# Two tables' pools become weight places from the third MLP on, and the loads of the S5 layer in another order

## The chip, the cores and the metric

The kernel runs on one core of a Trainium2 chip. The metric is the time of one execution on the device in microseconds, smaller is better. Five engines work beside each other, each through its own instructions in a fixed order: PE (matrix multiply; its weight loads are listed as PEld), DVE, ACT, POOL, and SP, which here only starts transfers. An instruction that has to wait holds back all that stands behind it on its engine.

## The reference

Four layers with a mixer each, and an MLP behind every mixer, on 256 tokens of 1024 channels, all in float32. The change touches the third MLP (`i = 2`) and the mixer after it, S5:

```python
for i in range(DEPTH):
    z = mixer_i(rmsnorm(h, norm_g[i, 0]))
    h = h + rmsnorm(z, norm_g[i, 1])
    z = rmsnorm(h, norm_g[i, 2])
    z = jnp.square(jax.nn.relu(z @ w_up[i])) @ w_down[i]
    h = h + rmsnorm(z, norm_g[i, 3])

def s5_mixer(h, ...):          # 64 groups of 16 channels, 64 complex states each
    bu_re, bu_im = ...         # u through the discretized input matrix
    _, _, xr, xi = lax.associative_scan(combine, (a_re, a_im, bu_re, bu_im), axis=1)
    y = einsum(xr, c_re) - einsum(xi, c_im) + d_skip * u
    y = gelu(y)
    return (y @ w_glu_a) * sigmoid(y @ w_glu_b)
```

## The kernel before

**Weights.** Every float32 product is made of three matmuls (`mm3`, all by line 297), so each weight is split into a high and a low part. A weight tile of 1 MB is loaded by SP (line 116) into one of three `raw` buffers. It is then split in two halves: ACT writes the high part (line 339), DVE the low part (line 340), both into a *place*, a buffer `w` of 8 KB per partition. There are `N_W = 8` places in a pool; a new split takes the place that was given out eight splits earlier, once PE is through with it. `Weights` keeps the order of the tiles (`stream` of each layer), starts the next load when a `raw` buffer has ended (`issue`), and `tick`, called after every unit of matmuls, starts a split when a place has come free by the planner's clock. A tile marked `plain` is not split. With `ahead=True` it is loaded straight into a place.

**The third MLP.** Eight groups `g` of 512 hidden channels: `up_units(g)` multiplies by `w_up` (96 matmuls of 128x256, tiles `mm`), `down_units(g - 1)` by `w_down` (48 matmuls of 128x512, tiles `acc`). A group's `w_up` are two tiles, so four places; so are its `w_down`.

**The tables.** S5's matrices are made on the device while the MLPs run, by a generator (`Tables.work`) whose steps are put between the other work. It uses two pools, `pre` (line 208) and `mp` (line 209). Its results go to DRAM: `d_e`, `d_m` and, in sixteen chunks, `d_f`. Each chunk of `d_f` is made by `into_maps`: six products on DVE (lines 1611 to 1616) from two loads (`pb`, `bt`), and a DMA from POOL's queue (line 1800). Chunks 6 to 15 come beside the third MLP; in `body`, `drain` runs what is left when `g == 6`, between `up_units(6)` and `down_units(5)`.

**S5.** There are four chunks `c` of 16 groups. `into(c)` multiplies by `d_f` chunk `c` and turns the result; `scan(c, v)` rotates it (line 1312), runs a scan in two halves (line 1352), rotates back, and sends it through four matmuls into `x` (line 1367); `within(c)` multiplies by `d_m` (line 1397), `out(c)` by `d_e`, and ACT applies the gelu (line 1409). `turn(0)`, after chunks 0 and 1, transposes and splits the result into `h1hi` and `h1lo`, and the GLU's matmuls can start on its first half. The `d_f` tiles go through the three `raw` buffers, the eight `d_m` and `d_e` through the eight places, and the GLU's weights come after all of them. A block of matmuls on zeros (tile `pf`, `keep_warm`) fills PE's wait ahead of S5.

The order on each engine is set at build time by a scheduler that lists the instructions by its own estimate of time.

Of the kernel before, what the change touches and what calls it, by code (L numbers as in the profile page):

```python
# [31 lines left out]

N_W = 8
N_RAW = 3
LAG = 2.0
# [32 lines left out]
class Tile:  # L68
# [3 lines left out]
    def __init__(self, ap, scale=None, plain=False, shape=None, load=None, ahead=False, gains=None, soon=False):  # L72
        self.gains, self.soon = gains, soon
        self.ap, self.scale, self.plain, self.load, self.ahead = ap, scale, plain, load, ahead
        self.shape = a, b = shape or ap.shape[1:]
        per = max(1, 1024 // b)
        self.cuts = [] if plain else [(i, min(per, a - i)) for i in range(0, a, per)]
        self.raw = None
        self.ended = False
        self.done = 0  # L80
        self.w = []


class Weights:
# [4 lines left out]
    def __init__(self, k):  # L89
# [3 lines left out]
        self.issued = self.current = self.taken = self.started = 0  # L93
        self.freed = []
        self.in_raw = []
# [21 lines left out]

    def place(self):
        self.started += 1
        return self.k.wp.tile([128, 2, 1024], F32R, name="w")  # L120

    def skip_plain(self):

        while self.current < len(self.tiles) and self.tiles[self.current].plain:
            t = self.tiles[self.current]
            if t.ahead:
                if self.started - N_W >= len(self.freed):
                    return
                self.load(t, self.place().bitcast(F32).rearrange("p a b -> p (a b)"))
            self.current += 1  # L130

    def ready(self, clock):

        self.skip_plain()
        if self.current >= self.issued or self.tiles[self.current].plain:
            return False
        j = self.started - N_W
        return j < 0 or (j < len(self.freed) and self.freed[j] <= clock)

    def split(self):  # L140
# [3 lines left out]
        i, m = t.cuts[t.done]  # L144
        assert self.current < self.issued and self.started - N_W < len(self.freed), "weights wait for their own use"
        b = t.shape[1]
        w = self.place()[:, :, 0:m * b].rearrange("p n (a b) -> p n a b", b=b)
        hi, lo = w[:, 0], w[:, 1]
# [11 lines left out]
        self.splits.append(lo_inst.ins)  # L160
        t.w += [(hi[:, e], lo[:, e]) for e in range(m)]
        t.done += 1
        if t.done == len(t.cuts):
# [18 lines left out]
    def free(self, n):  # L182

        self.freed += [self.k.clock] * n

    def free_plain(self, t):
        t.ended = True
        if t.ahead:
            self.free(1)
        self.issue()  # L190


class Core:


    def __init__(self, ctx, tc, a):
# [10 lines left out]
        self.small = pool("small", 6)  # L207
        self.pre_p = pool("pre", 1)
        self.mp = pool("mp", N_MAPS)
        self.dram = pool("dram", 1, space=bass.MemoryType.DRAM)  # L210
        self.pacc = pool("pacc", 4, space=PSUM)
        self.pmm = pool("pmm", 3, space=PSUM)
        self.pf = pool("pf", 1, space=PSUM)
        self.clock = self.credit = self.resume = 0.0
        self.background = None
# [61 lines left out]

    def drain(self):
        while self.background is not None:
            self.step()  # L280

    def run(self, units, side=()):
# [977 lines left out]
class S5(Sublayer):  # L1260
# [10 lines left out]
    def stream(self):  # L1271
        k, add = self.k, self.k.weights.add
        for c in range(4):
            add(k.d_f[:, 16 * c:16 * c + 16], plain=True)
        for c in range(4):
            for maps in (k.d_m, k.d_e):
                add(maps[:, 16 * c:16 * c + 16], plain=True, ahead=True)
        for n in ("d_w_glu_b", "d_w_glu_a"):
            for i in range(0, 8, 2):
                add(rows(self.a[n])[:, i:i + 2], soon=n == "d_w_glu_b" and i < 4)  # L1280

# [23 lines left out]
    def body(self):  # L1305
# [79 lines left out]
        v[3] = into(3)  # L1385
        maps = [k.weights.take() for i in range(8)]
        ys = {}
# [61 lines left out]
        k.tick(1.0)  # L1449
        wb = four()  # L1450
        states(2)
# [536 lines left out]
```

## Time and profile before

| | us |
|---|---|
| time, median of 3 runs | 1065.2 (1063.49 to 1066.76) |
| the profiled execution | 1065.79 |
| its span on the core | 1064.0 |
| PE busy | 1006.6 (95%) |
| DVE, ACT, POOL busy | 746.5, 545.3, 299.6 |
| DMA | 241.30 MB at 227 GB/s |

The profiled execution's own time is its span and 1.8 us around it, and lies 0.6 us over the median. Busy is the time in which an engine has at least one instruction running. PEclk is the share of PE's full clock that was granted: 1.00 is 2.4 GHz, 0.50 is 1.2 GHz. In timelines a row begins with start and duration in us; xN says how many instructions were merged into it, and [t <-X] that the engine stood idle for t before it and what ended that.

### The profile page before, as it was taken

To read this page: it belongs to the slowest core of one execution; us is meant where nothing else is said; L and a number is where in the kernel's file an instruction comes from. 1 tells how busy PE (TensorE), PEld (TensorE's weight loads), DVE (VectorE), ACT (ScalarE), POOL (GpSimd) and SP (SyncE) were. 2 spreads that over 40 slices of the span, in tenths; PEclk is the share of its full clock that TensorE was granted. 3 is DMA by queue.
4 is the path that set the end of the run, shared out by engine and by line. 5 is a ranking of instruction groups with operands and counts; after the bars stand their busy time and mean duration, and the time that the engine had idled before them with its cause. 6 is when DMAs were issued, how large, how long until landed. Compare 5 with 4: busy or idle time off the path is not lost.

```text
span 1064.0 us, 16397 instructions
## 1 busy us (share of the span) xinstructions
PE 1006.6 (95%) x6403; PEld 883.5 (83%) x6403; DVE 746.5 (70%) x1133; ACT 545.3 (51%) x816; POOL 299.6 (28%) x456
## 2 busy tenths in 40 slices
PE   7998999999889999998799999999998999999996
PEld 5886999999679999997688798888966778999995
DVE  5788998856788866579865857666857686455563
ACT  5956545544554454445465654444633656354451
POOL 4010000002118999996600526661100000000000
PEclk9999999999999999999899999999999999999999
DMA  9785557567957877756750889979978454646531
GB/s 315 238 277 171 187 186 235 193 201 256 344 181 249 271 258 242 247 186 220 272 186 21 270 271 311 323 269 318 336 309 301 159 184 160 210 159 206 191 120 39
DMA packets 84589, 241.30 MB, mean 227 GB/s; under 512 B 7408, under 2 KB 9712, under 8 KB 82720
## 3 DMA queue, kind: packets, MB, share of 16 engines
q1 hardware_dynamic: 66192, 180.89, 49.3%
q0 software_dynamic: 17648, 58.78, 16.4%
q8 instruction: 50, 0.82, 0.3%
q10 hardware_dynamic: 672, 0.59, 0.2%
q14 instruction: 27, 0.22, 0.1%
HBM read 220.05 MB, written 28.57 MB: 234 GB/s over the span
## 4 chain that ended last, share of the span: by engine, by line
PE 71%; DVE 9%; DMA 7%; issue 5%; ACT 3%; POOL 3%; DVEq 0%; ACTq 0%; POOLq 0%
PE acc L297 36%; PE mm L297 33%; DVE w L340 3%; DMA d_lag<-lg 2%; DMA d_f<-f 1%; DMA bt<-in_k_bt 1%; DMA bc<-in_norm_g 1%; PE pf L297 1%; ACT w L339 1%; DVE w L338 1%; POOL lg L1861 1%; DVE h L402 1%; ACT junk L353 1%; DMA raw<-in_d_w_glu_b 1%; DMA pb<-d_pb 1%
## 5 line engine op out<-in xcount | busy, mean ns | idle before, releaser
L340 DVE TENSOR_TENSOR w<-raw,w 128x1024 fp32r<-128x1024 f32 (+2 forms) x306 | 379.9, 1266 | 125.4 <-ACT w L339 123.9
L339 ACT ACTIVATE w<-raw 128x1024 fp32r<-128x1024 f32 (+2 forms) x306 | 312.0, 1044 | 211.0 <-PE acc L297 113.4
L297 PE MATMUL acc<-w,h1hi 128*128 128x512 f32 x1280 | 395.2, 392 | 3.1 <-DVE w L340 1.6
L297 PE MATMUL mm<-zhi,w 128*128 128x256 f32 x1920 | 355.2, 284 | 4.0 <-DVE s L853 2.4
L297 PEld LDWEIGHTS mm<-zhi,w 128*128 128x128 f32 x1920 | 303.2, 192 | 7.0 <-DVE s L853 2.6
L297 PEld LDWEIGHTS acc<-w,h1hi 128*128 128x128 f32 x1280 | 238.6, 189 | 53.2 <-DVE w L340 2.5
L297 PE MATMUL mm<-zlo,w 128*128 128x256 f32 x960 | 272.2, 284 | 0.0
L297 PE MATMUL acc<-w,h1lo 128*128 128x512 f32 x640 | 247.7, 392 | 2.8 <-DVE h1lo L340 2.8
L297 PEld LDWEIGHTS mm<-zlo,w 128*128 128x128 f32 x960 | 184.7, 192 | 1.1
L297 PEld LDWEIGHTS acc<-w,h1lo 128*128 128x128 f32 x640 | 120.6, 188 | 29.6 <-DVE h1lo L340 4.1
L339 ACT ACTIVATE h1hi<-s 128x512 fp32r<-128x512 f32 x60 | 45.3, 757 | 57.6 <-DVE s L647 56.0
L646 ACT ACTIVATE s<-mm 128x512 f32<-128x512 f32 x56 | 33.2, 593 | 64.2 <-PE mm L297 62.6
L647 DVE TENSOR_TENSOR s<-s 128x512 f32<-128x512 f32 x56 | 42.7, 763 | 29.2 <-ACT s L646 29.1
L340 DVE TENSOR_TENSOR h1lo<-s,h1hi 128x512 fp32r<-128x512 f32 x60 | 49.7, 830 | 19.0 <-ACT h1hi L339 18.8
L398 DVE TENSOR_TENSOR t<-acc,bc 128x512 f32<-128x512 f32 x28 | 19.2, 688 | 42.4 <-ACT junk L353 42.4
L353 ACT ACTIVATE junk<-acc 128x512 bf16<-128x512 f32 x28 | 16.6, 594 | 59.8 <-PE acc L297 59.6
L297 PE MATMUL mm<-w,zhi 128*128 128x512 f32 x128 | 40.3, 396 | 4.1 <-DVE zlo L340 3.2
L297 PE MATMUL acc<-w,zhi 128*128 128x512 f32 (+2 forms) x128 | 39.0, 384 | 2.4 <-ACT w L337 1.7
L1774 POOL DMA_DIRECT2D d_e<-ec x64 | 40.4, 633 | 0.0
L1749 POOL TENSOR_TENSOR ec<-bo,pr 128x256 f32<-128x256 f32 x32 | 33.6, 1050 | 9.0 <-DMA bo<-in_k_c 8.9
L329 POOL DMA_DIRECT2D bc<-in_norm_g x15 | 8.2, 547 | 97.3 <-DVE v L363 35.2
L1749 POOL TENSOR_TENSOR tmp<-bo,pi 128x256 f32<-128x256 f32 x32 | 32.8, 1025 | 1.1
(318 smaller groups left out, 1067.9 us busy)
## 6 DMA issues: line engine op xcount, KB each, us to landing
raw<-in_w_up SPq DMA_DIRECT2D x64, 1024.0 KB, 5.5
raw<-in_w_down SPq DMA_DIRECT2D x64, 1024.0 KB, 5.2
bc<-in_norm_g POOLq DMA_DIRECT2D x15, 512.0 KB, 5.7
raw<-in_a_w_in SPq DMA_DIRECT2D x7, 1024.0 KB, 10.7
d_ec<-ec POOLq DMA_DIRECT2D x16, 288.0 KB, 2.6
ec<-d_ec POOLq DMA_DIRECT2D x16, 288.0 KB, 6.8
bt<-in_k_bt POOLq DMA_DIRECT2D x16, 256.0 KB, 5.5
raw<-in_a_w_out SPq DMA_DIRECT2D x4, 1024.0 KB, 5.7
```

The lines of the kernel that those rows point to most:

```text
L297: return self.nc.tensor.matmul(out, lhsT, rhs, start=start, stop=stop)
L338: return i, nc.vector.scalar_tensor_tensor(lo, src, gain, hi.bitcast(F32), op0=ALU.mult, op1=ALU.subtract)
L339: i = nc.scalar.activation(hi, src, AF.Copy)
L340: return i, nc.vector.tensor_tensor(out=lo, in0=src, in1=hi.bitcast(F32), op=ALU.subtract)
L353: self.nc.scalar.activation(self.junk[:, 0:x.shape[-1]], x, AF.Square, scale=scale, bias=shift, accum_out=ss[:, i:i + 1])
L398: nc.vector.tensor_tensor(tn, zn, gn, op=ALU.mult)
L402: nc.vector.scalar_tensor_tensor(hn, tn, q, hn, op0=ALU.mult, op1=ALU.add)
L646: nc.scalar.activation(s, state[f], AF.Relu)
L647: nc.vector.tensor_tensor(s, s, s, op=ALU.mult)
L1749: tt = lambda o, x, y, op: nc.gpsimd.tensor_tensor(o, x, y, op=op)
L1774: nc.gpsimd.dma_start(out=k.d_e[64 * r:64 * r + 64, 4 * ch + g:4 * ch + 4:2], in_=e[hs, :, r, 1:9].rearrange("p q i c -> p q (i c)"))
L1861: nc.gpsimd.tensor_copy(v[:, e, 4:7, e], t[:, 1:6:2])
```

## The change

Places become a number that can grow. When the tables are done, `drain` closes their two pools and opens a pool `more` of two places in the memory that they held; from there on two of every ten splits take a place of `more` and the other eight of the old pool. The bookkeeping of free places goes by place number, since `d_f` chunks now end in another order than they were taken. In S5 all `d_f` tiles go into places (`ahead=True`), so the `raw` buffers stay with split weights; the stream puts the GLU's first tile ahead of the last `d_m` and `d_e`, and `body` takes them in that order. The GLU's first tiles are no longer marked `soon`.

```diff
@@ Weights
+    def widen(self, n):
+        self.n, self.more, self.since = N_W + n, n, self.started
+
-    def place(self):
+    def place(self, t):
+        t.places.append(self.started)
+        pool = self.k.more if self.more and (self.started - self.since) % self.n < self.more else self.k.wp
         self.started += 1
-        return self.k.wp.tile([128, 2, 1024], F32R, name="w")
+        return pool.tile([128, 2, 1024], F32R, name="w")
...
     def free(self, n):
-        self.freed += [self.k.clock] * n
+        self.end(self.split_places[0:n])
+        del self.split_places[0:n]
+
+    def end(self, places):
+        self.ends.update((p, self.k.clock) for p in places)
+        while len(self.freed) in self.ends:
+            self.freed.append(max(self.ends[len(self.freed)], self.freed[-1] if self.freed else 0))
...
@@ Core
-        self.pre_p = pool("pre", 1)
-        self.mp = pool("mp", N_MAPS)
...
+        self.made = ctx.enter_context(ExitStack())
+        self.pre_p = self.made.enter_context(tc.tile_pool(name="pre", bufs=1))
+        self.mp = self.made.enter_context(tc.tile_pool(name="mp", bufs=N_MAPS))
...
     def drain(self):
         while self.background is not None:
             self.step()
+        self.made.close()
+        self.more = self.ctx.enter_context(self.tc.tile_pool(name="more", bufs=N_MORE))
+        self.weights.widen(N_MORE)
@@ S5.stream
+        plain = lambda maps, c: add(maps[:, 16 * c:16 * c + 16], plain=True, ahead=True)
+        glu = lambda n, i: add(rows(self.a[n])[:, 2 * i:2 * i + 2])
         for c in range(4):
-            add(k.d_f[:, 16 * c:16 * c + 16], plain=True)
-        for c in range(4):
-            for maps in (k.d_m, k.d_e):
-                add(maps[:, 16 * c:16 * c + 16], plain=True, ahead=True)
-        for n in ("d_w_glu_b", "d_w_glu_a"):
-            for i in range(0, 8, 2):
-                add(rows(self.a[n])[:, i:i + 2], soon=n == "d_w_glu_b" and i < 4)
+            plain(k.d_f, c)
+        for c in range(3):
+            plain(k.d_m, c)
+            plain(k.d_e, c)
+        glu("d_w_glu_b", 0)
+        plain(k.d_m, 3)
+        plain(k.d_e, 3)
+        for i in range(1, 4):
+            glu("d_w_glu_b", i)
+        for i in range(4):
+            glu("d_w_glu_a", i)
@@ S5.body
-        maps = [k.weights.take() for i in range(8)]
+        maps = [k.weights.take() for i in range(6)]
...
-        wb = four()
+        wb = k.weights.take()
+        maps += [k.weights.take() for i in range(2)]
+        wb = wb + k.weights.take()
```

In the program as built, three places move. The first is ACT in the third MLP, at the splits of the last group's `w_up` (`w_7292` to `w_7317` before, `w_7292` to `w_7322` after); in brackets stand the semaphores waited for, where DMASW are the transfers of POOL's queue, DMAHW those of SP's. Before:

```order
L339 ACTIVATE w_7292<-raw_7115 128x1024 [waits DMAHW1_49,PE_49,Activation_49]
L339 ACTIVATE w_7295<-raw_7115 128x1024 [waits PE_49,Activation_49]
L646 ACTIVATE s_7287<-mm_7237 128x512 [waits PE_49]
L339 ACTIVATE w_7300<-raw_7170 128x1024 [waits DMAHW2_49,DVE_49]
L339 ACTIVATE w_7317<-raw_7170 128x1024 [waits DVE_49]
L339 ACTIVATE h1hi_7175<-s_7287 128x512 [waits DVE_49]
```

After:

```order
L361 ACTIVATE w_7292<-raw_7115 128x1024 [waits DMAHW1_49,PE_49,Activation_49]
L361 ACTIVATE w_7295<-raw_7115 128x1024 [waits PE_49,Activation_49]
L668 ACTIVATE s_7287<-mm_7237 128x512 [waits PE_49]
L361 ACTIVATE w_7300<-raw_7170 128x1024 [waits DMAHW2_49,DVE_49]
L361 ACTIVATE h1hi_7175<-s_7287 128x512 [waits DVE_49]
L361 ACTIVATE w_7322<-raw_7170 128x1024 [waits DMASW3_49,DMASW4_49,DMASW2_49,DMASW5_49,DMASW1_49,DMASW6_49,DMASW0_49,DMASW7_49,DVE_49,Pool_49]
L361 ACTIVATE w_7327<-raw_7205 128x1024 [waits DMAHW3_49]
```

The last quarter of these weights is now the first tile in the memory of the tables' pools, and its split has moved behind `h1hi` and waits for all that used that memory.

The second is DVE in S5, from the second chunk's scan to the first half's `h1lo` (`s` are the scan's tiles, `w` splits). Before:

```order
L1352 SCALAR_TENSOR_TENSOR s<-t,s 128x256 x2
L1312 TENSOR_TENSOR s<-s,t 128x512 x2
L340 TENSOR_TENSOR w<-raw,w 128x1024
L1312 TENSOR_TENSOR s<-mm,t 128x512 x2
L340 TENSOR_TENSOR w<-raw,w 128x1024
L1312 TENSOR_TENSOR s<-s 128x256 x2
L1312 TENSOR_TENSOR s<-mm,t 128x512
L340 TENSOR_TENSOR w<-raw,w 128x1024
L340 TENSOR_TENSOR h1lo<-acc,h1hi 128x4x128 x2
```

After:

```order
L1380 SCALAR_TENSOR_TENSOR s<-t,s 128x256
L362 TENSOR_TENSOR w<-raw,w 128x1024
L1380 SCALAR_TENSOR_TENSOR s<-t,s 128x256
L362 TENSOR_TENSOR w<-raw,w 128x1024
L1340 TENSOR_TENSOR s<-s,t 128x512 x2
L1340 TENSOR_TENSOR s<-mm,t 128x512 x2
L1340 TENSOR_TENSOR s<-s 128x256 x2
L362 TENSOR_TENSOR w<-raw,w 128x1024
L1380 SCALAR_TENSOR_TENSOR s<-t,s 128x256 x2
L1340 TENSOR_TENSOR s<-mm,t 128x512
L362 TENSOR_TENSOR w<-raw,w 128x1024
L1340 TENSOR_TENSOR s<-s,t 128x512 x2
```

Two GLU splits now stand inside the second chunk's scan, and behind the rows shown follow one more split and then `h1lo`, with the third chunk's scan ahead of it.

The third is SP's queue around S5. Before:

```order
L116 DMA raw<-d_f 128x2048 x3
L116 DMA w<-d_m 128x2048
L116 DMA w<-d_e 128x2048
...
L116 DMA raw<-d_f 128x2048
L116 DMA raw<-in_d_w_glu_b 128x2x1024 x4
```

After:

```order
L119 DMA raw<-in_d_w_glu_b 128x2x1024 x2
L119 DMA w<-d_f 128x2048 x2
L119 DMA raw<-in_d_w_glu_b 128x2x1024
L119 DMA w<-d_f 128x2048 x2
L119 DMA w<-d_m 128x2048
L119 DMA w<-d_e 128x2048
...
L119 DMA raw<-in_d_w_glu_b 128x2x1024
```

Three of the four tiles of `d_w_glu_b` are now loaded ahead of the maps.

## Rows read from the trace of the kernel before

**Rows 1.** The page, part 1: busy us, share of the span, instructions.

```profile
PE 1006.6 (95%) x6403; PEld 883.5 (83%) x6403; DVE 746.5 (70%) x1133; ACT 545.3 (51%) x816; POOL 299.6 (28%) x456
```

**Rows 2.** Stretches: us, then busy us (instructions) by engine, PEclk, DMA share, GB/s.

```profile
740.00:760.00 20.00, 20.00 (x126) 18.11 (x126) 18.77 (x25) 12.71 (x14) 4.11 (x8) 1.00 0.89 305
780.00:800.00 20.00, 18.54 (x176) 12.05 (x178) 13.81 (x34) 7.11 (x17) 0.62 (x2) 1.00 0.99 403
800.00:820.00 20.00, 16.06 (x255) 12.01 (x248) 15.07 (x23) 8.22 (x14) 0.00 (x0) 1.00 0.81 306
```

**Rows 3.** The chain that ended last, in order of time: start, us, what.

```profile
753.17 11.51 PE mm L297 x96
764.68 21.79 PE acc L297 x96
805.40 6.35 DMA raw<-in_d_w_glu_b
```

**Rows 4.** Timeline of ACT in the third MLP's last groups.

```profile
747.38 2.20 ACT L339 ACTIVATE w<-raw 128x1024 fp32r<-128x1024 f32 x2
749.49 1.18 ACT L339 ACTIVATE h1hi<-s 128x512 fp32r<-128x512 f32 x1
```

**Rows 5.** Timeline of DVE there.

```profile
749.02 2.34 DVE L340 TENSOR_TENSOR w<-raw,w 128x1024 fp32r<-128x1024 f32 x2
751.29 0.41 DVE L1612 TENSOR_TENSOR t<-pb,bt 128x256 f32<-128x256 f32 x1
754.28 0.42 DVE L1616 TENSOR_TENSOR f<-f,t 128x256 f32<-128x256 f32 x1
```

**Rows 6.** Timeline of POOL there: the last chunk of d_f.

```profile
755.00 0.55 POOL L1800 DMA_DIRECT2D d_f<-f  x1 [9.69 <-DVE f L1616]
```

**Rows 7.** DMA issues of d_f at 755.0, 648.1, 709.8: KB, us from issue to landing.

```profile
d_f<-f POOLq DMA_DIRECT2D x1, 256.0 KB, 4.5
d_f<-f POOLq DMA_DIRECT2D x1, 256.0 KB, 3.9
d_f<-f POOLq DMA_DIRECT2D x1, 256.0 KB, 6.9
```

**Rows 8.** Timeline of PE ahead of the first MLP, and stretches as in Rows 2.

```profile
294.10 2.31 PE L297 MATMUL mm<-zhi,t 128*128 128x128 f32 x10 [3.98 <-DVE t L430]
290.00:295.00 5.00, 1.02 (x6) 0.90 (x6) 4.54 (x13) 4.91 (x12) 0.00 (x0) 0.93 1.02 406
295.00:300.00 5.00, 5.00 (x30) 4.90 (x30) 4.96 (x9) 1.29 (x3) 0.55 (x1) 0.72 0.73 244
```

**Rows 9.** Timeline of PE in S5.

```profile
800.67 1.06 PE L1397 MATMUL pf<-w,zlo 128*32 128x128 f32 x32
807.18 1.08 PE L297 MATMUL mm<-s,ident 128*64 128x256 f32 x8 [0.37 <-DVE s L1312]
812.24 0.66 PE L1333 MATMUL mm<-ident,s 128*128 128x128 f32 x4 [1.19 <-ACT s L1329]
814.16 1.20 PE L297 MATMUL acc<-w,h1hi 128*128 128x512 f32 x4 [0.34 <-ACT h1hi L339]
817.40 0.50 PE L297 MATMUL acc<-w,h1lo 128*128 128x512 f32 x1 [2.04 <-DVE h1lo L340]
```

**Rows 10.** Timeline of ACT in S5.

```profile
804.36 0.65 ACT L1367 ACTIVATE t<-mm 128x248 f32<-128x248 f32 x2 [6.09 <-PE mm L297]
805.47 0.60 ACT L1329 ACTIVATE s<-mm 128x512 f32<-128x512 f32 x1 [0.46 <-PE mm L297]
809.69 2.00 ACT L339 ACTIVATE w<-raw 128x1024 fp32r<-128x1024 f32 x2
```

**Rows 11.** Timeline of DVE in S5.

```profile
805.04 1.27 DVE L1352 TENSOR_TENSOR_SCAN s<-t,s 128x256 f32<-128x256 f32 x2
806.34 1.29 DVE L1312 TENSOR_TENSOR s<-s,t 128x512 f32<-128x512 f32 x2
```

**Rows 12.** Timeline of PE at the fourth MLP's start.

```profile
881.89 0.73 PE L297 MATMUL mm<-w,zhi 128*128 128x512 f32 x2 [0.70 <-DVE zlo L340]
```

More of the change, by code (lines that the diff above doesn't have):

```diff
@@ L33 @@
 N_W = 8
+N_MORE = 2
 N_RAW = 3
@@ L78, in __init__ @@
         self.raw = None
+        self.places = []
         self.ended = False
@@ L93, in __init__ @@
         self.issued = self.current = self.taken = self.started = 0
-        self.freed = []
+        self.freed, self.ends, self.split_places = [], {}, []
+        self.n, self.more, self.since = N_W, 0, 0
         self.in_raw = []
@@ L126, in skip_plain @@
             if t.ahead:
-                if self.started - N_W >= len(self.freed):
+                if self.started - self.n >= len(self.freed):
                     return
-                self.load(t, self.place().bitcast(F32).rearrange("p a b -> p (a b)"))
+                self.load(t, self.place(t).bitcast(F32).rearrange("p a b -> p (a b)"))
             self.current += 1
@@ L136, in ready @@
             return False
-        j = self.started - N_W
+        j = self.started - self.n
         return j < 0 or (j < len(self.freed) and self.freed[j] <= clock)
@@ L144, in split @@
         i, m = t.cuts[t.done]
-        assert self.current < self.issued and self.started - N_W < len(self.freed), "weights wait for their own use"
+        assert self.current < self.issued and self.started - self.n < len(self.freed), "weights wait for their own use"
         b = t.shape[1]
-        w = self.place()[:, :, 0:m * b].rearrange("p n (a b) -> p n a b", b=b)
+        w = self.place(t)[:, :, 0:m * b].rearrange("p n (a b) -> p n a b", b=b)
         hi, lo = w[:, 0], w[:, 1]
@@ L161, in split @@
         t.w += [(hi[:, e], lo[:, e]) for e in range(m)]
+        self.split_places.append(t.places[-1])
         t.done += 1
@@ L182, in free @@
     def free(self, n):
-        self.freed += [self.k.clock] * n
+        self.end(self.split_places[0:n])
[4 more added lines that the diff above has]
+            self.freed.append(max(self.ends[len(self.freed)], self.freed[-1] if self.freed else 0))
     def free_plain(self, t):
         t.ended = True
-        if t.ahead:
-            self.free(1)
+        self.end(t.places)
         self.issue()
@@ L213, in __init__ @@
         self.pf = pool("pf", 1, space=PSUM)
+        self.made = ctx.enter_context(ExitStack())
+        self.pre_p = self.made.enter_context(tc.tile_pool(name="pre", bufs=1))
+        self.mp = self.made.enter_context(tc.tile_pool(name="mp", bufs=N_MAPS))
+        self.ctx = ctx
         self.clock = self.credit = self.resume = 0.0
```

## The prediction, made before the changed kernel ran

> **What bounds the kernel now.** First the page's busy times: PE is busy for 95% of the span, the next engine for 70% [rows 1], so time is gained or lost almost only where PE stands still or runs slowly. Then the stretches: in the third MLP's last groups PE is busy for 20.00 of 20 us, in S5 it stands still for 1.46 us of one stretch and 3.94 us of the next [rows 2]. Then the chain that ended last, to see what PE waits for in each place. In the third MLP it is PE itself, 11.51 us for the last group's up product and 21.79 us for the down products behind it, without a gap; in S5 it runs through the load of the GLU's weights [rows 3]. The timelines of the engines there carry the sum.
>
> **A wait where there was none: the third MLP.** The first split that goes into the new memory is the last quarter of the last group's `w_up`, `w_7322`. As built it waits for the tables' pools to be empty, and the last to leave is the DMA that writes the sixteenth chunk of `d_f`: the count waited for on DMASW4 is the one that this DMA raises. When does it land? Before, DVE's products for that chunk begin at 751.29 and the last begins at 754.28 [rows 5]; POOL issues the DMA at 755.00 [rows 6], and it lands 4.5 us later [rows 7], at 759.5. The change takes one low part (2.34 / 2 = 1.17 us [rows 5]) out of DVE's way ahead of these products, but `h1lo` now precedes them and waits for `h1hi`, which follows on ACT when the one high part left of the 2.20 us pair is done [rows 4]. I take 0.9 us earlier: issue at 754.1, landing at 758.6.
>
> PE gets to the last group at 753.17 and takes 11.51 / 96 = 0.120 us a matmul [rows 3]. As built, 18 matmuls stand ahead of the first on `w_7322`, so PE stops at 753.17 + 18 x 0.120 = 755.3. ACT's split takes 2.20 / 2 = 1.1 us [rows 4], so PE goes on at 758.6 + 1.1 = 759.7. **The wait is 4.4 us**, on a stretch in which PE was the chain, so all of it counts. For landing the nearest rows are 3.9 and 6.9 us [rows 7], so the wait is 3.8 to 6.8; I take 4.5, the same chunk's own row. The Trainium skill, "DMA: Bandwidth & Descriptors", section "Anatomy of one DMA — SWDGE (gpsimd) path", gives such a DMA a fixed 2.0 us and its bytes at 436 GB/s, an estimate of 2.6 us for 256 KB; by that the wait would be 2.5 us and the sum 1.9 us smaller. No d_f row of the trace is that short, so the rows decide.
>
> Behind `w_7322` on ACT stand the splits of both last `w_down` pairs and the relu of this group. They are late, but not late enough for a second wait: from 759.7 ACT and DVE need about 1.15 us for each part, the four of the next down product are through at about 765.5, and PE wants them at 764.68 + 4.4 = 769.1. The loads behind them on SP start only when `w_7322`'s `raw` buffer is free, at about 760.9; the splits of the last pair then fall into 767 to 773, and PE wants them 24 matmuls of 21.79 / 96 = 0.227 us after 769.1, at 774.6. That cover is about 1 us at its thinnest (the last `h1hi`, at about 774.5, is wanted 11 matmuls later).
>
> **What the wait does to PE's clock.** After standing still for 3.98 us PE goes on at 294.10 and the granted clock is 0.93 in that stretch and 0.72 in the next [rows 8]; 5 x 0.07 + 5 x 0.28 = 1.75 us of PE's time are lost to the lower of the two levels. A wait of 4.4 us is longer, so I add **1.7 us** (between none, as after the 2.04 us wait in S5, where the stretch shows 1.00 [rows 2, 9], and twice this, if a further wait falls into the slow time).
>
> **The GLU's weights in S5.** What can be gained: ahead of the GLU PE waits 1.19, 0.34 and 2.04 us [rows 9], 3.6 us in all, for ACT and DVE, which have the first GLU splits to make when the load has landed at 811.8 [rows 3]. After the change these weights are there long before. But the order then puts two splits into the second chunk's scan, and that scan is itself on the way to the GLU. In times of before, to which the wait above has to be added: the third chunk's `within` (1.06 us for one, about 0.9 from start to start) no longer stands ahead of the first chunk's last matmuls [rows 9], so the chain starts 0.9 us earlier. ACT copies `x` at 804.36 - 0.9 = 803.5 for 0.65 us, then `s` for 0.5 [rows 10], so it is free at 804.65 and splits until 805.65 (2.00 / 2 [rows 10]). DVE has done the first half of the scan at 804.14 + 0.64 = 804.8 [rows 11], waits for that split, makes its low part (1.15), the second half (0.64), the second split's low part (1.15) and the first product (0.65): 805.65 + 3.6 = 809.25. PE started on this product at 807.18 [rows 9]: **2.0 us later**, and PE stands still for about 3.2 us there.
>
> From there the way to the GLU holds on DVE, as built: six products and a scan for the third chunk (1.3 + 0.7 + 0.65 + 1.3 and 1.27), three more low parts (3 x 1.15) and one `h1lo` (0.65), 9.3 us, and some 1.5 us of waiting for PE's matmuls and ACT's copy, from 809.9 to 820.7. Before, the GLU went on at 817.40 [rows 9], with 2.0 us of the third chunk's matmuls still to do, which after the change are done by then. So the GLU is 820.7 - 817.4 - 2.0 = **1.3 us later**, not 3.6 us earlier. Bounds: the whole 3.6 us gained, or 3 us lost if the half-speed clock and the waits add up. The 3.2 us wait can lower the clock as the one in rows 8 did; part of the slow time lies under ACT and DVE, which set the pace there, so of 1.7 us I count **1.0** (0 to 1.7).
>
> **Edits at nothing.** The third and fourth `d_f` tiles now load when places of the next to last down product come free: 769.1 + 63 x 0.227 = 783.4, ahead of the `d_m` and `d_e`. At the 403 GB/s of [rows 2] a tile of 1 MB takes 2.6 us; the seventh, the third chunk's `d_m`, is there at about 802 and wanted at about 808. If that cover went, each tile late would cost its 2.6 us. The new bookkeeping is done at build time.
>
> **Two places ahead later.** At the fourth MLP's start PE waits 0.70 us for a low part [rows 12]; as built, four down matmuls (4 x 0.227 = 0.9 us) now stand in that gap, their weights being two splits further on: **-0.7 us** (0 to -0.7). Elsewhere in that MLP each split waits for the same use as before, so nothing else moves.
>
> **The sum.** 4.4 + 1.7 + 1.3 + 1.0 - 0.7 = +7.7 us. The profiled execution took 1065.8, so 1073.5; it lies 0.6 over the median of 1065.2, so against the median **1072.9**.
>
> **The rivals.** (1) It does what it is described to do and nothing waits: the splits of the GLU no longer hold PE, -3.6 - 0.7 = -4.3, so 1061. It needs `d_f`'s last chunk to have landed by 755.3 - 1.1 = 754.2, the time at which it is issued; the shortest landing of [rows 7] is 3.9. Only if DVE's products for it ran some 4 us earlier would that decide. For it speaks that DVE's order there is mended by one part; against it all of rows 5 to 7. (2) The wait in the third MLP stands, but S5 gains what rows 9 offer: 4.4 + 1.7 - 3.6 - 0.7 = +1.8, so 1067, no change that can be told. It is decided by DVE in the second chunk: if the first product is there by 807.2 (plus 4.4), as before. Against it stands the order, for it that I have the times of ACT and DVE there only by adding rows. (3) The wait is at its long end, a landing of 6.9 us [rows 7] (+2.4), and the clock falls twice at full price (+0.7), or a low part misses its cover of 1 us (+1): 1077.
>
> **How the numbers follow.** About 0.3%, 3.2 us, is what a measurement of this kernel can tell from no change. Forecast (1070 to 1075.5) 0.60, rival 1 0.06, rival 2 0.18, rival 3 0.16. Faster is rival 1, 0.06; the same is rival 2, 0.18; slower the rest, 0.76. The range leaves out rival 1 and the ends of the others: 1066.5 to 1077.5.
>
> **What would show it.** On ACT, the second split of the pair ahead of `h1hi` gone and a wait of some 8 us for a transfer before the next split, ended by the DMA of `d_f`; on PE, a gap of 4 to 5 us after 18 matmuls of the last group and a granted clock under 1.00 behind it. In S5, DVE's scan halves torn apart by low parts and a PE wait of 3 us ahead of the second chunk's `mm<-s,ident`; the waits charged to GLU splits smaller. Wrong would be: no PE gap before 765 (the whole forecast falls), a gap under 3 us (the landing was mis-sized), or S5 shorter from the end of the zeros to the second `turn` than before.

## The result, and the profile of the changed kernel

The changed kernel takes 1071.25 us (median of 20 runs, 1061.68 to 1077.63), the kernel before 1064.22 us beside it (20 runs). The profiled execution's span is 1069.5 us. The ratio is 1.0052, 95% interval 1.0034 to 1.0070: slower by 5.5 us; the two medians lie 7.0 apart. Twelve more runs gave 1.0046 (1.0021 to 1.0072). The forecast was +7.7 us, 1072.9. Two runs on record are in a slow state, 1077.63 us of the changed kernel and 1630.09 us of the one before; the ratios and the table of the clock below leave them out.

**The third MLP.** First PE's timeline in the last up product (start, us, engine, line, operation, count, then the idle time ahead and who ended it), then ACT, DVE and POOL beside it, and the DMA's issue to landing. These answer [rows 3 to 7].

```profile
746.16 0.28 PE L319 MATMUL mm<-zhi,w 128*128 128x256 f32 x1
...
748.20 0.28 PE L319 MATMUL mm<-zhi,w 128*128 128x256 f32 x1
752.36 0.58 PE L319 MATMUL mm<-zhi,w 128*128 128x256 f32 x1 [3.88 <-ACT w L361]
```

```profile
743.65 1.23 ACT L361 ACTIVATE h1hi<-s 128x512 fp32r<-128x512 f32 x1 [0.67 <-DVE s L669]
751.25 2.00 ACT L361 ACTIVATE w<-raw 128x1024 fp32r<-128x1024 f32 x2 [6.37 <-DMA d_f<-f]
```

```profile
744.91 1.14 DVE L362 TENSOR_TENSOR h1lo<-s,h1hi 128x512 fp32r<-128x512 f32 x1 [0.16 <-ACT h1hi L361]
745.95 0.43 DVE L1642 TENSOR_TENSOR t<-pb,bt 128x256 f32<-128x256 f32 x1
...
747.88 0.43 DVE L1646 TENSOR_TENSOR f<-f,t 128x256 f32<-128x256 f32 x1
```

```profile
748.61 0.55 POOL L1830 DMA_DIRECT2D d_f<-f  x1 [8.81 <-DVE f L1646]
```

```profile
d_f<-f POOLq DMA_DIRECT2D x1, 256.0 KB, 2.3
```

PE gets through its 18 matmuls and stands still for 3.88 us. ACT has waited since `h1hi` for the sixteenth chunk of `d_f`, splits `w_7322`, and PE goes on. What then happens to the clock is in the stretches (us, then busy us and instructions of PE, weight loads, DVE, ACT and POOL, granted clock, DMA share, GB/s), three here and three of S5:

```profile
745.00:750.00 5.00, 3.47 (x24) 3.04 (x22) 3.24 (x7) 0.00 (x0) 1.39 (x3) 1.00 0.53 204
750.00:755.00 5.00, 2.64 (x12) 2.65 (x13) 2.66 (x3) 3.28 (x4) 0.89 (x3) 0.57 0.92 297
755.00:760.00 5.00, 5.00 (x35) 5.00 (x34) 3.32 (x3) 1.90 (x2) 0.00 (x0) 0.75 1.03 410
...
805.00:810.00 5.00, 2.27 (x36) 1.56 (x30) 4.15 (x6) 2.43 (x3) 0.00 (x0) 0.87 0.95 305
810.00:815.00 5.00, 5.00 (x36) 2.66 (x32) 1.44 (x3) 0.00 (x0) 0.00 (x0) 0.50 0.90 310
815.00:820.00 5.00, 3.65 (x58) 2.53 (x56) 3.76 (x7) 4.62 (x8) 0.00 (x0) 0.94 0.05 17
```

The up product takes 17.87 us from its first matmul to the first of the down product, 11.51 before: 3.88 of standing still and 2.5 of lower clock (0.50 is 1.2 GHz, 1.00 is 2.4 GHz).

**S5.** DVE in the second chunk's scan, and the two places where PE then waits:

```profile
804.38 0.68 DVE L1380 TENSOR_TENSOR_SCAN s<-t,s 128x256 f32<-128x256 f32 x1
805.91 1.23 DVE L362 TENSOR_TENSOR w<-raw,w 128x1024 fp32r<-128x1024 f32 x1 [0.85 <-ACT w L361]
807.05 0.68 DVE L1380 TENSOR_TENSOR_SCAN s<-t,s 128x256 f32<-128x256 f32 x1
807.65 1.20 DVE L362 TENSOR_TENSOR w<-raw,w 128x1024 fp32r<-128x1024 f32 x1
808.77 1.29 DVE L1340 TENSOR_TENSOR s<-s,t 128x512 f32<-128x512 f32 x2
```

```profile
809.60 1.98 PE L319 MATMUL mm<-s,ident 128*64 128x256 f32 x8 [2.73 <-DVE s L1340]
...
824.12 0.50 PE L319 MATMUL acc<-w,h1lo 128*128 128x512 f32 x1 [0.39 <-DVE h1lo L362]
```

The scan is torn by two low parts, PE stands still for 2.73 us, and the 2.04 us that PE waited for `h1lo` [rows 9] have shrunk to 0.39: the wait moved ahead and grew. With two places more, more splits also fall into S5: from the zeros to the GLU's second half (the stretch in the table below) DVE makes 12 low parts, in both traces, where it made 9 before.

**The fourth MLP's start.** PE, where the prediction wanted four down products in a gap:

```profile
887.14 1.18 PE L319 MATMUL acc<-w,h1hi 128*128 128x512 f32 x4 [0.92 <-ACT h1hi L361]
```

They stand there, but do not fill the gap: they wait for `h1hi` for 0.92 us, where the products of [rows 12] waited 0.70.

PE's time by stretch, worked out from the starts in the timelines of two traces of each kernel:

| stretch of PE, us | before | after |
|---|---|---|
| first matmul to the third MLP's last up product | 749.0, 749.5 | 741.2, 748.3 |
| last up product | 11.5, 11.5 | 17.9, 17.3 |
| last down product, to the zeros | 21.8, 22.0 | 22.0, 22.3 |
| zeros to the GLU's second half (its first `h1lo` product) | 52.3, 52.0 | 57.4, 55.8 |
| to the down products behind the fourth MLP's second up product | 60.8, 60.8 | 62.1, 62.1 |
| to PE's end | 156.5, 156.5 | 156.0, 156.0 |

From the last up product on, the changed kernel is 12.5 and 10.5 us longer than the mean of the two traces of before, while its runs are 5.5 us longer. The first row is shorter, by 8.1 us in the first trace, though up to its last instructions this part of the program is the same in both kernels. There it is the clock: by the granted clock of each 5 us, 6.8 us were lost in that stretch, against 13.7 in each trace of before and 15.3 in the second trace of the changed kernel. What the clock does over many runs is in the experiments.

### The profile page after: what moved, and what is told of

It is laid out like the page before. It is cut to its first block, busy times and chain, and to the rows that moved or that the text cites. A ratio compares the mean times of both kernels' runs of the same rounds, so it can differ in the third digit from the quotient of the medians.

```text
span 1069.5 us, 16407 instructions
## 1 busy us (share of the span) xinstructions
PE 1008.4 (94%) x6403; PEld 881.4 (82%) x6403; DVE 744.9 (70%) x1133; ACT 545.9 (51%) x816; POOL 297.7 (28%) x456
## 5 line engine op out<-in xcount | busy, mean ns | idle before, releaser
L361 ACT ACTIVATE h1hi<-s 128x512 fp32r<-128x512 f32 x60 | 45.8, 764 | 53.6 <-DVE s L669 52.0
L420 DVE TENSOR_TENSOR t<-acc,bc 128x512 f32<-128x512 f32 x28 | 19.2, 689 | 43.5 <-ACT junk L375 43.5
L319 PE MATMUL mm<-w,zlo 128*32 128x128 f32 (+1 forms) x192 | 31.9, 334 | 2.0 <-DVE zlo L362 2.0
```

Source lines behind the costliest of these rows:

```text
L319: return self.nc.tensor.matmul(out, lhsT, rhs, start=start, stop=stop)
L361: i = nc.scalar.activation(hi, src, AF.Copy)
L420: nc.vector.tensor_tensor(tn, zn, gn, op=ALU.mult)
```

## The experiments

Two theories to begin with. **A**: two separate losses, the wait for the tables' last transfer in the third MLP and the torn scan in S5. **B**: one of them is an accident of one execution, or what one gives back the other takes. Each kernel ran 12 times (one, named below, 9 times), each set beside runs of the kernel before on the same chip.

**The changed kernel again** (no edit).

> The changed kernel itself, once more, for a second trace beside the first. Theory A (both places of the prediction are real and repeat): PE stands still for 3.9 us after 18 of the last up product's 96 matmuls in the third MLP, as in the first trace, and for 2.7 us ahead of the second chunk's products in S5; from the start of the last up product to the start of the zeros block 39.9 us, from there to the second h1lo product of the GLU 57.4 us (before: 33.1 and 52.3). Theory B (one of the two is an accident of one execution): one of these four numbers comes out within 1 us of its value before. Either way the total is 1067 to 1075 us. Whether the slow clock behind both gaps repeats is open: in the first trace it took 3.4 us in each place.

Measured: 1.0046 (1.0021 to 1.0072), median 1066.74 against 1063.73. PE's wait was 3.16 us instead of 3.88, and S5's 2.73 again:

```profile
757.72 0.58 PE L319 MATMUL mm<-zhi,w 128*128 128x256 f32 x1 [3.16 <-ACT w L361]
```

Both places repeat, so A. But a median 4.5 us lower than in the first set, with the same waits, says that something else differs between runs or sets of runs.

**The new places later.**

```diff
+    n = property(lambda self: N_W + (self.more if self.started >= self.since else 0))
     def widen(self, n):
...
-        self.n, self.more, self.since = N_W + n, n, self.started
+        self.more, self.since = n, self.started + 9
...
-        pool = self.k.more if self.more and (self.started - self.since) % self.n < self.more else self.k.wp
+        pool = self.k.more if self.n > N_W and (self.started - self.since) % self.n < self.more else self.k.wp
```

> The two new places are first used nine places later, from the first d_f tile on, so no split of the third MLP goes into the tables' memory; S5's order stays that of the changed kernel. Theory A (the third MLP's wait is the one for the tables' last transfer): no gap in the last up product, that stretch back to 33.1 us, 3.9 us of waiting and up to 3.4 us of slow clock gone; S5 unchanged at +5; total 1071 - 4 to - 7.3, so 1064 to 1067, within 0.3% of the kernel before. Theory B (the gap is made by the late loads or the order of ACT, not by the tables): a gap over 2 us stays in the third MLP and the total stays over 1069.

Measured: 1.0032 (1.0007 to 1.0057), median 1066.73. The last up product takes 11.51 us again: the tables' memory was the cause of the wait there. But 1.51 us came back further on. PE's timeline, and the waits of SP's queue from 740 to 780 us (total, times, longest):

```profile
772.50 0.96 PE L319 MATMUL acc<-w,h1hi 128*128 128x512 f32 x3 [1.51 <-ACT h1hi L361]
```

```profile
SPq L119 <- DMA d_f<-f: 5.8, 1, 5.8
```

SP now waits for the same transfer, with the loads of the first two `d_f` tiles, and the last `w_down` tile stands behind them in its queue. S5 stayed as in the changed kernel (9.07 us from the first scan's products to the second's in both).

**No split inside the first two scans.**

```diff
-        states(0)
+        k.hold = True; states(0)
         v[2] = into(2)
         states(1)
-        v[3] = into(3)
+        v[3] = into(3); k.hold = False
```

> The changed kernel with no split of weights made while the first two scans of S5 are emitted, so that the second chunk's scan stands in one piece on DVE; the third MLP's wait stays. Theory A (the torn scan is what costs in S5): PE's gap ahead of the second chunk's products falls from 2.7 to about 0.4 us, the slow clock behind it goes, and from the zeros block to the second h1lo product of the GLU it is 47 to 50 us instead of 57.4 (before 52.3); total 1062 to 1066. Theory B (DVE has too much to do there whatever the order, and the wait only moves to h1lo behind the third scan): that stretch stays over 54 us and the total over 1068.

Measured: 1.0002 (0.9973 to 1.0031), median 1063.41. The third MLP's wait is there (2.79 us). In S5 the scan is whole and the gap ahead of its products gone, but the next chunk's is torn and `zhi` comes late. DVE, then PE:

```profile
806.24 1.26 DVE L1380 TENSOR_TENSOR_SCAN s<-t,s 128x256 f32<-128x256 f32 x2
```

```profile
815.50 1.09 PE L1447 MATMUL acc<-ident,zhi 128*128 128x128 f32 x8 [1.51 <-ACT zhi L1437]
```

From the zeros to the GLU's second half it took 53.7 us, none of it at the lower clock: between the two theories, 2 to 4 us back and nothing gained on before. Nearly all that came back is slow clock: the changed kernel's two traces without their slow clock have 54.0 (below), so the tear as such is worth 0.3 us, and 1.5 us over before stay. The 12 low parts of the stretch are still there. That is the first sign that the early load was not what S5 lacked.

**Both edits.**

> Both edits at once: the new places used from the first d_f tile on, and no split inside the first two scans. Theory A (two independent losses): 1071 - 4 to 7 - 5 to 8, so 1056 to 1062, faster than the kernel before by 0.3 to 0.8%. Theory B (the losses hide each other, or what is freed is lost again to the slow clock): 1063 or more, no different from the kernel before.

Measured: 1.0011 (0.9986 to 1.0036), median 1064.71; S5 52.7 us. By the total B, but a look at the third MLP says why: the tile of `w_down` that SP held back came later still. ACT, then PE:

```profile
771.31 2.00 ACT L361 ACTIVATE w<-raw 128x1024 fp32r<-128x1024 f32 x2 [7.32 <-DMA raw<-in_w_down]
```

```profile
774.40 1.65 PE L319 MATMUL acc<-w,h1hi 128*128 128x512 f32 x3 [3.30 <-ACT h1hi L361]
```

**Both edits, the places two later still** (`self.started + 11`), so that only the third and fourth `d_f` tile use them. Their loads were meant to come when `w_down` is on its way.

> As the run with both edits, but the new places are first used two places later still, by the third and fourth d_f tile, so that the loads of the first two d_f tiles no longer stand on SP ahead of the last w_down tile. Theory A (the 3.3 us gap in the last down product came from w_down queued behind loads that wait for the tables): no gap over 0.5 us from the last up product to the zeros block, 33.3 us for it; S5 52.7 us as in that run; total 1062 to 1064.5, no different from the kernel before. Theory B (that gap has another cause): a gap over 1 us in the last down product again and a total over 1064.5.

Measured: 1.0024 (0.9999 to 1.0050), median 1067.55. The gap in the down product is down to 0.72 us, between the two theories, and the kernel is not better than before. PE, then SP's waits from 740 to 780 us and its queue:

```profile
771.54 0.97 PE L319 MATMUL acc<-w,h1hi 128*128 128x512 f32 x3 [0.72 <-ACT h1hi L361]
```

```profile
SPq L119 <- DMA d_f<-f: 6.7, 1, 6.7
```

```profile
756.29 1.60 SPq L119 DMA_DIRECT2D w<-d_f  x2
758.00 0.40 SPq L119 DMA_DIRECT2D raw<-in_w_down  x1
```

The edit did not do what it was for. As built, the two loads ahead of the last `w_down` tile are now those of the third and fourth `d_f` tile, with the same waits for the tables' transfers, so SP is held again, for 6.7 us. That `w_down` is late because of the queue is read from the traces (SP held, ACT waiting for that tile, PE for ACT); no run took the loads out of its way. The three gaps of 1.51, 3.30 and 0.72 us came with `w_down` in the same place of SP's queue, behind two `d_f` loads.

**The kernel before again, and the clock.**

> The kernel before, once more, for a second trace and for the granted clock of more of its runs. Theory A (the slow clock costs both kernels alike over many runs, wherever it falls): the share of the span lost to the lower clock is 16 to 17 us here as in the changed kernel's 32 runs, and the stretches are 11.5 us for the last up product, 52.3 us from the zeros block to the second h1lo product of the GLU, within 0.5. Theory B (the first trace of before was an odd one): a gap of over 1 us in the last up product, or a stretch off by over 1 us.

Measured: median 1064.24, the stretches within 0.5 us of the first trace. Each run comes with its span and its mean granted clock. Span x (1 - clock) is what the lower clock takes off (the time behind PE's last matmul included), and span x clock the time that would be left at full clock. Medians over all runs of a kernel on record with their clock:

| kernel | runs | lost to the lower clock, us | time at full clock, us |
|---|---|---|---|
| before | 124 | 17.0 | 1045.6 |
| changed | 31 | 16.0 | 1050.8 |
| places later | 12 | 16.0 | 1050.0 |
| no split inside two scans | 12 | 14.8 | 1048.2 |
| both | 12 | 15.9 | 1048.1 |
| both, two later still | 12 | 16.5 | 1049.4 |
| own places (below) | 12 | 16.5 | 1046.6 |
| own places and hold (below) | 24 | 14.8 | 1045.9 |
| three own places (below) | 24 | 14.8 | 1043.5 |
| changed, narrow again (below) | 9 | 19.2 | 1049.8 |

The means for before and changed are 16.7 and 16.5 (standard error 0.2 and 0.6). So **the lower clock costs the changed kernel no more than the one before**, although both of its new gaps are followed by a slow stretch in each of its traces. The measure is rough for a single run: the clock is recorded to 0.001, a step of 1.06 us, in which the medians of the third column move, and one run of three own places has a clock of 0.948 at a span of 1060.4 us, which would be 55 us lost. Over the 124 runs of before it holds: the span grows by 0.96 us for each us lost. If the changed kernel loses some 5 us behind its new gaps (6.9 and 5.2 in its traces from the last up product on, 0.1 and 0.2 before), it must lose as much less elsewhere. The traces show one such place: both traces of before are slow behind their waits at 719, the changed kernel's two are not. The first two lines are the stretch from 720 us of before and of its second trace, the third that of the changed kernel:

```profile
720.00:725.00 5.00, 4.80 (x14) 3.83 (x15) 3.76 (x7) 3.43 (x4) 1.94 (x4) 0.66 1.02 263
```

```profile
720.00:725.00 5.00, 4.49 (x13) 3.26 (x12) 3.75 (x6) 2.69 (x3) 3.16 (x5) 0.66 1.00 314
```

```profile
720.00:725.00 5.00, 5.00 (x31) 4.46 (x30) 4.34 (x5) 2.52 (x3) 0.00 (x0) 1.00 0.95 357
```

Why that slow stretch is missing there, with up to 1.6 us of waits in the same place, is open.

**Own places.** If not the load, what does the GLU wait for? A new theory **C**: for `h1lo`, and that for the low parts that stand ahead of it on DVE. The kernel before in its S5 order, with the tables' memory as two places for the two splits of the GLU's first tile, outside the ring. Those are made in the third MLP's tail.

```diff
+        if t.own:
+            t.places.append(None)
+            return self.k.more.tile([128, 2, 1024], F32R, name="w")
...
+        for i in range(0, 2, 2):
+            add(rows(self.a["d_w_glu_b"])[:, i:i + 2], own=True)
         for c in range(4):
             add(k.d_f[:, 16 * c:16 * c + 16], plain=True)
```

> The kernel before in its S5 order, with the tables' memory as two places for the two splits of the first GLU tile alone, outside the ring; they are made behind the last h1lo of the third MLP, where DVE and ACT stand idle. Theory A (in S5 DVE's sum of work ahead of the GLU sets the end, so only work that leaves the stretch counts): no wait in the third MLP, two low parts of 1.15 us less ahead of the GLU, from the zeros block to the second h1lo product 50 to 51.5 us (before 52.3), total 1061 to 1063. Theory B (the order and the transposes set it, not the sum): 52 us or more, total 1063 to 1065.

Measured: 1.0019 (0.9996 to 1.0042), median 1065.25. DVE in the third MLP's tail, then DVE and PE ahead of the GLU:

```profile
768.72 2.38 DVE L364 TENSOR_TENSOR w<-raw,w 128x1024 fp32r<-128x1024 f32 x2
```

```profile
807.61 1.22 DVE L364 TENSOR_TENSOR w<-raw,w 128x1024 fp32r<-128x1024 f32 x1 [3.15 <-ACT w L363]
...
809.95 1.22 DVE L364 TENSOR_TENSOR w<-raw,w 128x1024 fp32r<-128x1024 f32 x1
...
812.35 1.22 DVE L364 TENSOR_TENSOR w<-raw,w 128x1024 fp32r<-128x1024 f32 x1
813.48 1.28 DVE L364 TENSOR_TENSOR h1lo<-acc,h1hi 128x512 fp32r<-128x512 f32 x2
```

```profile
814.22 0.79 PE L321 MATMUL acc<-w,h1lo 128*128 128x512 f32 x1 [2.05 <-DVE h1lo L364]
```

The two low parts are made ahead of S5, no wait came in the third MLP, and PE waits 2.05 us for `h1lo` as before (2.04 [rows 9]): the scheduler has put the next tile's splits into the empty room, three ahead of `h1lo` as before. From the zeros to the GLU's second half it took 53.6 us, of which the lower clock took up to 1.7, so 51.9 or more, and DVE made 9 low parts there, as before. So this run does not test the sum: DVE's work in the stretch stayed what it was, and so did the time. The next two tell the sum from the order.

**Own places, and a hold** from the first scan until the third chunk's `within`, so that two splits and not three stand ahead of `h1lo`:

```diff
-        states(0)
+        k.hold = True; states(0)
...
-        k.run([(lambda: within(2), 1.2)])
+        k.run([(lambda: within(2), 1.2)]); k.hold = False
```

> As the run before it, and no split is made from the first scan until the third chunk's products are emitted, but the two that the GLU's first half needs; so two splits instead of three stand ahead of h1lo on DVE. Theory A (DVE's sum): another 1.15 us less, 49 to 50.5 us from the zeros block to the second h1lo product, total 1060 to 1062, faster than the kernel before. Theory B: as the run before it, within 0.5 us.

> The run with two own places and the hold, once more, since its gain is near what can be told. Theory A (a low part less ahead of h1lo is 1.1 us of PE, and what else the first set of runs gained is a share of slow clock by chance): a ratio of 0.997 to 1.000, median 1061 to 1063.5 us; in the trace again 9.1 us from the second chunk's products to the GLU's first h1lo product, 10.2 before. Theory B (the shorter wait also saves slow clock for good): 0.994 to 0.997, and 13 to 14 us lost to the lower clock where before loses 16 to 17.

Measured: 0.9965 (0.9939 to 0.9992), median 1060.21, and once more 0.9984 (0.9965 to 1.0002), 1061.55. In both traces PE's wait is half:

```profile
810.45 1.23 DVE L364 TENSOR_TENSOR w<-raw,w 128x1024 fp32r<-128x1024 f32 x1 [3.15 <-ACT w L363]
...
812.79 1.22 DVE L364 TENSOR_TENSOR w<-raw,w 128x1024 fp32r<-128x1024 f32 x1
...
815.19 1.28 DVE L364 TENSOR_TENSOR h1lo<-acc,h1hi 128x512 fp32r<-128x512 f32 x2
```

```profile
811.90 0.66 PE L1359 MATMUL mm<-ident,s 128*128 128x128 f32 x4 [1.19 <-ACT s L1355]
...
815.93 0.50 PE L321 MATMUL acc<-w,h1lo 128*128 128x512 f32 x1 [1.00 <-DVE h1lo L364]
```

One low part less ahead of `h1lo` is 1.05 us of PE's wait, and the stretch from the zeros is 51.1 us in both traces, 0.9 to 1.2 below before, with the 9 low parts of before in it: the order on DVE decides, not the sum of its work. The totals do not show this 1 us: at full clock these runs are no shorter than before (means of 1045.6 and 1045.7, standard errors 0.4 and 0.2), so by this measure their whole gain lies in the clock, 14.0 us lost against 16.7 in the mean (standard errors 0.5 and 0.2). Why this order should get less of the lower clock is open, and the second set's interval reaches no change.

**Three own places**: a third for the third split of the GLU's first half.

```diff
-N_MORE = 2
+N_MORE = 3
...
+        add(rows(self.a["d_w_glu_b"])[:, 2:3], own=True)
```

> Three own places: the third holds the third split of the GLU's first half, so one low part instead of two stands ahead of h1lo on DVE, and half of the third scan (0.64 us) has moved ahead of it. Theory A (what stands ahead of h1lo on DVE sets the GLU's start): 0.5 to 1.1 us less than with two own places, 8.0 to 8.6 us from the second chunk's products to the first h1lo product, total 1060 to 1062. Theory B (h1lo is by now held by PE's transposes and ACT's h1hi, DVE has slack): as with two own places within 0.3 us.

> The run with three own places once more, to see whether its gain stands. Theory A (1.8 us of PE's waiting ahead of the GLU's first h1lo product are gone and 0.7 us come back ahead of the second, so 2.2 us at full clock with what the first half saves; the rest of the first result is the clock's): a ratio of 0.996 to 0.999, with 7.3 us again from the second chunk's products to the first h1lo product. Theory B (the gain was chance): the interval holds 1.000 in its middle.

Measured: 0.9963 (0.9944 to 0.9982), median 1059.87, and 0.9976 (0.9959 to 0.9992), 1060.70. DVE and PE:

```profile
809.52 1.23 DVE L364 TENSOR_TENSOR w<-raw,w 128x1024 fp32r<-128x1024 f32 x1 [1.76 <-ACT w L363]
812.54 0.67 DVE L364 TENSOR_TENSOR h1lo<-acc,h1hi 128x512 fp32r<-128x512 f32 x1
```

```profile
810.03 0.66 PE L1362 MATMUL mm<-ident,s 128*128 128x128 f32 x4 [0.24 <-ACT s L1358]
...
813.26 0.50 PE L321 MATMUL acc<-w,h1lo 128*128 128x512 f32 x1 [0.21 <-DVE h1lo L364]
...
834.00 1.20 PE L321 MATMUL acc<-w,h1hi 128*128 128x512 f32 x4 [1.06 <-ACT h1hi L363]
```

With one split ahead of `h1lo`, on ACT too, both waits for S5's splits are gone (1.19 to 0.24, 2.04 to 0.21); 0.7 us come back ahead of the GLU's second half. The gain from the second chunk's products to the GLU was 2.9 us (10.22 to 7.34), more than expected, since I had counted DVE alone. From the zeros to the GLU's second half it is 50.1 us, 1.9 to 2.2 below before, again with 9 low parts, and the time at full clock is 2.1 below. This version beats the kernel before in both sets, and with it the changed kernel.

**The changed kernel, eight places again from the fourth MLP on.**

```diff
+    def narrow(self, t):
+        if t.narrow and self.more:
+            self.n, self.more = N_W, 0
```

> The changed kernel, with the ring of weights back at eight places from the first weights of the fourth MLP on; all ahead of that as changed. Theory A (the two places more are what the fourth MLP loses by: four down products go ahead of the second up product, at the end of its gap and not in it): 217.2 us from the GLU's second h1lo product to PE's end, as before, where the changed kernel takes 218.1; total 0.8 us below the changed kernel's, 1066 to 1070. Theory B (the 0.8 us comes from the S5 side, by other times of loads): 218 us in that stretch.

Measured: 1.0084 (1.0055 to 1.0113), median 1071.51. The four hoisted products are gone and the last stretch is 156.47 us, as before, but by the total this is not better than the changed kernel: it lost 19.2 us to the lower clock. From the GLU's second half to PE's end its trace has 219.9 us (217.2 and 218.1 were the expected values), up to 3.4 of them lost to the lower clock, so the stretch does not decide either. At full clock it has 1049.8 against 1050.8, which would fit the 0.8 us, but nine runs do not tell 1 us. The trace had something else to show. The order ahead of S5 is the changed kernel's, and ACT waits for `d_f` as there, but PE does not wait. PE, then ACT:

```profile
750.34 0.28 PE L323 MATMUL mm<-zhi,w 128*128 128x256 f32 x1
```

```profile
748.62 2.01 ACT L365 ACTIVATE w<-raw 128x1024 fp32r<-128x1024 f32 x2 [6.37 <-DMA d_f<-f]
```

PE started this product at 747.95 here, 2.0 us after POOL had issued the last chunk (745.98); in the changed kernel's traces 2.45 and 1.72 us ahead of that. So the wait in the third MLP is a race between the tables' chain and PE, and comes out at 3.88, 3.16, 2.79 and 0 us in four traces of one order.

## Why the prediction was right, point by point

The time (1071.25 against 1072.9), the sign and the places were right, the closeness of the time in part by luck: the second set of the changed kernel has a median of 1066.74, 3.0 us above the kernel before beside it. Of the terms, one was right as a sum of two errors, one had the wrong sign, and one does not exist over many runs.

- **The wait in the third MLP, 4.4 us: 3.88, 3.16, 2.79 and once 0.** The mechanism stood as described: 18 matmuls, then PE waits for ACT, ACT for the sixteenth chunk, and without that memory there is no gap in the up product. Both parts of the size were off, with opposite signs, so that the size came out near is luck.

The first part is the time of issue. I had it 0.9 us behind PE's first product of the last group. It came 2.45, 1.72 and 1.35 us behind and once 1.97 ahead, and in the two traces of before 1.99 and 3.34 behind. DVE's work up to the last product did get 0.9 us shorter, as I had it: from 743.54 to 748.31 is 4.77 us, where before it was 5.68, from 749.02 [rows 5] to 754.70. But `h1lo` did not move as I said. Before, it already stood ahead of five of the six products, which [rows 5] do not show:

```profile
751.62 1.16 DVE L340 TENSOR_TENSOR h1lo<-s,h1hi 128x512 fp32r<-128x512 f32 x1
```

What failed is that I took where this work begins, as seen from PE, from one trace of before: it began 3.99 us ahead of PE's product there, 2.63 in the second trace of before, and 2.62, 3.36, 3.69 and 7.08 in the four traces of the changed order.

The second part is the landing, 4.5 us by [rows 7]; it was 2.3 in all four traces of this order. The step that failed was to take a transfer's landing from a row at another time, when the DMA engines had other work. The stretches are the us up to the issue, here and before, then SP's wait here from 746 to 754 us:

```profile
747.60:748.60 1.00, 0.87 (x8) 0.67 (x6) 0.67 (x2) 0.00 (x0) 0.00 (x0) 1.00 0.04 16
```

```profile
754.00:755.00 1.00, 1.00 (x11) 1.00 (x10) 0.97 (x3) 0.00 (x0) 0.00 (x0) 1.00 0.98 381
```

```profile
SPq L119 <- DVE w L362: 10.1, 1, 10.1
```

The DMA share is 0.04 here and 0.98 before: the late split holds back the `raw` buffers, SP has nothing to start for 10.1 us, and the transfer has the DMA engines nearly to itself. In the us ahead of the issue the share is 0.03 to 0.06 in the four traces with 2.3 us, and 0.93 to 1.03 in the ten others, where this transfer took 2.7 to 4.5, 3.1 in the second trace of before. So the 4.5 of [rows 7] was also the longest of ten. The estimate after the Trainium skill, "DMA: Bandwidth & Descriptors", section "Anatomy of one DMA — SWDGE (gpsimd) path", 2.6 us, agrees with this trace's 2.3 better than my rows did.

- **The clock, +1.7 and +1.0: seen in the traces, absent from the runs.** Behind both gaps the granted clock is low, and each time it costs what I said or more (2.5 us in the up product). But over 31 and 124 runs the loss to the lower clock is 16.5 and 16.7 us in the mean. The step that failed is the addition: a kernel that loses 17 us to slow stretches in many places does not lose that much more for each gap that is added, and I had looked at one place at a time.
- **S5, +1.3: +1.8 at full clock.** The torn scan came as the order said, with a gap of 2.73 us (3.2 forecast), and the wait for `h1lo` shrank. That the tear is what costs the 1.8 us is not shown: with the scan in one piece 53.7 and 52.7 us were left. From 57.4 and 55.8 us I take off what the granted clock took in those stretches, 3.4 (5 x 0.13 + 5 x 0.50 + 5 x 0.06) and 1.7, which leaves 54.0 both times, against 52.2 before. Rival 2, that S5 gains 3.6 us, fell: even with the scan in one piece S5 gained nothing.
- **The fourth MLP, -0.7: +0.8.** The four products are hoisted, but they need `h1hi`, which ends the gap that they were to fill. I had looked at their weights only. The stretches give +1.25 and -0.5. The run with eight places there removed the hoist: its stretch ahead of these down products is 63.4 us, of which the lower clock took up to 3.4, so 60.0 or more, and its last one 156.5. That points to the hoist; its total did not show the difference.
- **Edits at nothing** held: PE nowhere in S5 waits for a map.

At full clock the terms are about 3.3 + 1.8 + 0.8 = 5.9 us (the first the mean of the three waits; 5.1 with the fourth trace's 0), and the time at full clock rose by 5.2, with a race among them that PE sometimes wins. Taking the two causes away gave back less: 0.8 us with the places later, 2.6 without splits in two scans, 2.7 with both (table; by the means 0.9, 2.9 and 2.9, with a standard error of 0.9 each). Part of it came back as the late `w_down`, and where the rest of S5's loss lies is open. The forecast of +7.7 was 2 us above the measured +5.5; without the 2.7 us of its clock terms it would have been +5.0.

## What to carry to other kernels

Memory that is handed from one use to another carries the slowest DMA of the old use with it: count from when that lands, on every queue whose next instruction touches the memory, SP's too, and give it first to something that is needed late. Weights that are there early gain nothing when the scheduler fills each empty place on the vector engine with the next split: count what stands ahead of the critical instruction, not how much work the stretch holds; one low part less there was worth 1.05 us of PE's wait, while two that were made ahead of the stretch were worth nothing, because two others took their room. Take a landing from a row with the traffic that the transfer will meet after the change, and the meeting of two engines from more than one trace. Before a gap is charged with a slow clock as well, compare the clock of many runs of both kernels.

## What the runs showed of the hardware

- The loss to the lower clock differs between programs by more than their gaps explain: 14.8 (own places and hold), 17.0 (before) and 19.2 us (narrow again) in the median for three that differ in a few instructions, while the changed kernel with two more gaps loses no more than the one before. What decides it is open.
- The same 256 KB transfer took 2.3 us to land in the four traces in which the DMA engines' share was 0.03 to 0.06 in the us ahead of its issue, and 2.7 to 4.5 us in the ten with 0.93 to 1.03.
- Two engines in one order can meet in either sequence: the tables' last transfer was issued between 2.45 us behind and 1.97 us ahead of PE's product in four traces.
